# An encoder trunk on one core: widths of the FFNs' parts, pauses of the modulation sums, a second operand made from a copy, and row loads at another place

## The chip, the cores and the metric

The kernel runs on one core of a Trainium2 chip, in one launch. The metric is the time of an execution on the device in microseconds (us), as the median of several runs. The engines are named as in the profile: PE is TensorE (PEld its weight loads), DVE is VectorE, ACT is ScalarE, POOL is GpSimd, SP is SyncE, which here issues nearly all DMAs.

## The reference

A sequence of 256 positions of width 1024 passes two layers of three sub-layers each. Each sub-layer modulates its input with a scale and a shift that depend on a vector c, applies f, adds the result times a gate to the residual and normalises:

```
mod = silu(c) @ w_ada[l] + b_ada[l]              # nine vectors of 1024 per layer
h = x * (1.0 + scl) + shift
x = layer_norm(ALPHA * x + w * gate * f(h), ln_g, ln_b)
```

The six f are, in order: a SwiGLU FFN (0,0), a gMLP with a 128x128 position mixing, an FFN (0,1); then an FFN (1,0), an attention over chunks, an FFN (1,1). An FFN is `(silu(g) * u) @ w_down` with g, u the halves of `h @ w_gu`, 1024 to 2 x 2816 to 1024. Behind FFN (0,1) the residual stream is modulated a second time, with other vectors, into the operand from which attention's keys and values are made. Everything is float32.

## The kernel before, in words

**Split operands.** A float32 matmul is made from three fp32r matmuls: with x = xh + xl and w = wh + wl the kernel adds xh wh, xh wl and xl wh (`mm_unit`, L268). So every weight tile of 128 x 1024 (a unit) is loaded by a DMA (`load_raw`, L130; six buffers), cast by ACT (`hi`, L216) and subtracted by DVE (`lo`, L226). The 328 units stand in one list, `stream`, in the order of their use.

**Tiles and ticks.** The 256 rows are two row tiles t of 128. A pass (`gemm_pass`, L309) runs one row tile over 4, 6, 8 or 2 units; the same units then serve row tile 1. One unit for one row tile is six matmuls of 512 columns, and behind them comes a *tick* (L295). An FFN (`ffn`, L627) is cut into parts of columns of its inner width: for each part it makes the activations in chunks of 512 or 256 columns (`gu_part`, L483), then multiplies them by their rows of `w_down` (`down`, L611, in pieces of up to eight units) and adds the product to the residual X (`add_y`, L384, on DVE). An FFN has 132 ticks, 16 for a chunk of 512, 8 for one of 256, two for a unit of `w_down`; the gMLP has 96, attention 64; of the first FFN the first two chunks run in a form of their own, without ticks of this kind. The last piece of eight units runs with one half of the columns after the other (`half`), in 16 ticks called quiet.

**The planner.** All engines' orders are written out by hand while the ticks are counted. A tick runs what `after(n, fn)` has put off by n ticks, then makes as many lo (with their loads and casts) as the lead of six units (eight in the last piece) asks for (`prep`, L230), bounded by 11 unit buffers, then perhaps one *sum* (`run_sums`, L193). A sum is one eighth of a modulation vector: a 512 KB load on SP and a multiply with accumulation on DVE (`column`, L140, one instruction and a short read of the accumulator). There are 144, in the order of `SUMS`; when they run is set by the pairs (ticks, rate) given to `step` (L923): each tick adds its rate to a credit capped at 2; a tick that made a lo needs a credit of 2 for a sum, another one of 1; a quiet tick runs none. `need` (L198) runs missing sums at once, where a vector is wanted. A finished gate goes through DRAM and comes back as a row tile, loaded on SP.

**A seam** is where one sub-layer ends and the next begins. At the end of a row tile DVE adds, makes statistics, normalises (`end_sublayer`, L447); 4.5 or 5 ticks later PE transposes half of X (`make_h`, L363), ACT makes hf = A x + B from PSUM in four pieces and casts it to the operand's high part, DVE subtracts for the low part (hl, L333, `modulated`, L350); the other half follows two ticks later. Row tile 0 ends eight ticks ahead of the seam. The residual itself gets its LayerNorm rows g and b later, in two pieces of two DVE operations (`residual_affine`, L433), `LAG_R` ticks behind the second half. At the end of FFN (0,1) `make_h` has two sets to make, for hT and for hkT (attention's key and value operand), one right after the other. The rows g and b (two loads of 512 KB on SP, `load_lnrow`, L424) are loaded in `next_affine` (L914), in front of the last down piece.

**After a chunk** ACT applies Silu (sg, L475), one tick later DVE multiplies (a, L479), three ticks later PE transposes the product (tp, L344), ACT casts it and DVE subtracts (th, tl).

In the trace the sub-layers begin at about 0, 202, 351, 542, 738 and 862 us.

Of the kernel before, what the change touches and what calls it, by code (L numbers as in the profile page):

```python
# [8 lines left out]
F32 = mybir.dt.float32  # L9
# [5 lines left out]
P = 128  # L15
# [4 lines left out]
D_FF = 2816  # L20
# [12 lines left out]
ENDS = [HALVES, (0, 512, 768, 1024)]  # L33
# [8 lines left out]
LAG_A = 3  # L42
LAG_H = (4.5, 5)
LAG_H2 = 2
LAG_R = ((12, 16), (12, 16))
LAG_S = 1
LAG_HL = 2
LAG_T = 1.5
LAG_V = ((5, 8, 28, 32), (5, 9, 30, 36))

# [16 lines left out]
def encoder_kernel(ctx, tc, a, out):  # L67
    nc = tc.nc
# [8 lines left out]
    bigp = pool("bigp", N_BIG)  # L77
# [172 lines left out]
    def row_units(w, k0, nk, c0=0):  # L250
        return [lambda raw, k=k: [(raw, w[k * P:(k + 1) * P, c0:c0 + D])]
                for k in range(k0, k0 + nk)]

    def gu_units(w, c0, wd):
        wv = w.rearrange("k (s f) -> k s f", s=2)
        if wd == 512:
            return [lambda raw, k=k: [(raw.rearrange("p (s n) -> p s n", s=2),
                                       wv[k * P:(k + 1) * P, :, c0:c0 + 512])] for k in range(KD)]

        def two(raw, k):  # L260
            rv = raw.rearrange("p (q s n) -> p q s n", q=2, s=2)
            return [(rv[:, q], wv[(k + q) * P:(k + q + 1) * P, :, c0:c0 + 256]) for q in range(2)]
        return [lambda raw, k=k: two(raw, k) for k in range(0, KD, 2)]
# [24 lines left out]
    def after(n, fn, early=False):  # L288
        late.append([n, fn, early])
# [60 lines left out]
    def modulated(tp, A, B, js, p, tag, store, lag):  # L350

        w = len(js) * P
        hf = sgp.tile([P, 512], F32, tag="sg", name=nm("hf"))
        for i, j in enumerate(js):
            sl = slice(i * P, (i + 1) * P)
            nc.scalar.activation(hf[:, sl], tp[:, sl], AF.Identity,  # L356
                                 bias=B[:, j:j + 1], scale=A[:, j:j + 1])
        hi = p.tile([P, 512], F32R, tag=tag, name=nm("hh"))
        lo = p.tile([P, 512], F32R, tag=tag, name=nm("hl"))
        split4(hf[:, :w], (hi[:, :w], lo[:, :w]),  # L360
               lambda: store.extend(tiles4(hi, lo, len(js))), lag)

    def make_h(t, half, mods_):  # L363

        js = range(half * 4, half * 4 + 4)
        tp = pt.tile([P, 512], F32, tag="pt", name=nm("hp"))
        for i, j in enumerate(js):
            nc.tensor.transpose(tp[:, i * P:(i + 1) * P], X[t][:, j * P:(j + 1) * P], ident)  # L368
        for i, (A, B, p, tag, store) in enumerate(mods_):
            modulated(tp, A, B, js, p, tag, store[t], LAG_HL + 1.5 * i)  # L370

    def affine(scl, shift, ln):

# [26 lines left out]
    def pieces(x_, cuts):  # L400
        return [x_[:, c0:c1] for c0, c1 in zip(cuts, cuts[1:])]
# [20 lines left out]
    lnrow = {}  # L422

    def load_lnrow(ln):  # L424
        g = rowp.tile([P, D], F32, tag="lng", name=nm("lng"))
        b = rowp.tile([P, D], F32, tag="lnb", name=nm("lnb"))
        nc.sync.dma_start(out=g, in_=a["ln_g"][ln:ln + 1, :].partition_broadcast(P))
        nc.sync.dma_start(out=b, in_=a["ln_b"][ln:ln + 1, :].partition_broadcast(P))
        lnrow[ln] = (g, b)
# [1 line left out]
    waiting = [[], []]  # L431

    def residual_affine(t, ln):  # L433
        g, b = lnrow[ln]

        def part(sl):
            nc.vector.tensor_tensor(X[t][:, sl], X[t][:, sl], g[:, sl], op=ALU.mult)
            nc.vector.tensor_tensor(X[t][:, sl], X[t][:, sl], b[:, sl], op=ALU.add)
            waiting[t].remove(sl)
        waiting[t] = [slice(i * 512, (i + 1) * 512) for i in range(2)]  # L440
        for lag, sl in zip(LAG_R[t], waiting[t]):
            after(lag, lambda sl=sl: part(sl))
# [4 lines left out]
    def end_sublayer(t, stats, ln, nxt):  # L447

        mu, rs = stats.rstd()
        for x_ in pieces(X[t], HALVES):  # L450
            nc.vector.tensor_scalar(x_, x_, mu, rs, op0=ALU.subtract, op1=ALU.mult)
        hT[t] = []
        after(LAG_H[t], lambda: make_h(t, 0, nxt["mods"]))

        def second():
            make_h(t, 1, nxt["mods"])
            residual_affine(t, ln)
        after(LAG_H[t] + LAG_H2, second)

    def last_y(t, gate, first, done, cuts=HALVES):  # L460
# [166 lines left out]
    def ffn(l, i, gate, done, before_last, parts, start=None, cuts=(HALVES, HALVES)):  # L627
        for pi, part in enumerate(parts):
            aT = [[], []]
            if start and pi == 0:  # L630
                first_gu_part(a["ffn_gu"][l, i], part[:2], aT)
                start()
                gu_part(part[2:], aT)
            else:
                gu_part(part, aT)
            last = pi == len(parts) - 1
            down(sum(w for _, w in part) // P, aT, gate, pi == 0,
                 done if last else None, before_last if last else None,
                 cuts if last else (HALVES, HALVES))

    def ffn_stream(l, i, parts, skip=0):

        for pi, part in enumerate(parts):
            for c0, wd in part[skip if pi == 0 else 0:]:
                stream.extend(gu_units(a["ffn_gu"][l, i], c0, wd))
            stream.extend(row_units(a["ffn_down"][l, i], part[0][0] // P,
                                    sum(w for _, w in part) // P))

    PARTS1 = [[(c, 512) for c in (0, 512, 1024)], [(1536, 512), (2048, 512), (2560, 256)]]
    PART_A = [(0, 512), (512, 256)]  # L650
    PARTS2 = [PART_A, [(c, 512) for c in range(768, D_FF, 512)]]
# [103 lines left out]
    def transposed(accs, scale, name, store):  # L755
# [7 lines left out]
        for n in range(2):  # L763
            s_ = sgp.tile([P, 512], F32, tag="sg", name=nm(name))
            nc.scalar.mul(s_, accs[n], scale)
            after(LAG_T + n, lambda n=n, s_=s_: turn(n, s_))

# [4 lines left out]
    def attention(gate, done, before_last):  # L772
# [43 lines left out]
        def scores(t, hs):  # L816
# [22 lines left out]
            def second():  # L839
# [4 lines left out]
                st[(t, hs)] = pr  # L844
            after(LAG_T, second)

# [67 lines left out]
    def next_affine(ln, nxt, *keys):  # L914

        def f():
            need(*(k for ks in keys for k in ks))
            nxt["mods"] = [affine(mods[s_], mods[b_], ln) + dst
                           for (s_, b_), dst in zip(keys, ((htp, "h", hT), (bigp, "b", hkT)))]
            load_lnrow(ln)  # L920
        return f

    def step(ln, *rate):  # L923

        ada["rate"] = list(rate)
        nxt = {}
        return lambda t, stats: end_sublayer(t, stats, ln, nxt), nxt
# [10 lines left out]
    def start():  # L938
        for lag, fn in ((12, lambda: load_x(0)), (18, lambda: load_x(1)), (40, load_small)):
            after(lag, fn)  # L940

    ffn_stream(0, 0, PARTS1, 2)
    gmlp_stream()
    ffn_stream(0, 1, PARTS2)
    ffn_stream(1, 0, PARTS3)
    attention_stream()
    ffn_stream(1, 1, PARTS2)

    with tc.manual_schedule(engines={ET.SP, ET.PE, ET.DVE, ET.Activation, ET.Pool}):
        done, nxt = step(0, (6, 0), (16, 0.55), (0, 0.38))  # L950
        ffn(0, 0, (0, 2), done, next_affine(0, nxt, ((0, 4), (0, 3))), PARTS1, start=start)
        done, nxt = step(1, (4, 0), (16, 0.3), (24, 0), (0, 0.34))
        gmlp((0, 5), done, next_affine(1, nxt, ((0, 7), (0, 6))))
        done, nxt = step(2, (4, 0), (16, 0.5), (0, 0.34))
        ffn(0, 1, (0, 8), done, next_affine(2, nxt, ((1, 1), (1, 0)), (("kv", 1), ("kv", 0))), PARTS2)
        done, nxt = step(3, (4, 0), (16, 0.45), (0, 0.24))
        ffn(1, 0, (1, 2), done, next_affine(3, nxt, ((1, 4), (1, 3))), PARTS3)
        done, nxt = step(4, (4, 0), (0, 0.4))
        attention((1, 5), done, next_affine(4, nxt, ((1, 7), (1, 6))))
        step(5, (2, 0), (0, 0.8))  # L960
        ffn(1, 1, (1, 8), final, lambda: load_lnrow(5), PARTS2, cuts=ENDS)


# [38 lines left out]
```

## Time and profile before

| | |
|---|---|
| median of 3 runs | 1062.37 us (1062.26 to 1067.6) |
| the profiled execution | 1062.69 us |
| its span, first to last instruction | 1060.9 us |
| mean granted clock of TensorE | 0.996 |
| matmuls and weight loads | 4774 each |
| DMA | 285.74 MB, mean 269 GB/s |
| loads of units and sums | 160 of w_cols (sums), 160 and 32 of ffn_gu, 88 of ffn_down, 80 of the other weights |

The profile is of one execution. Busy time of an engine is the union of its instructions. Matmuls overlap each other and so do the instructions of DVE and ACT by some 0.1 us, so the cost of an instruction in a full queue is read from start to start. A wait is idle time of an engine, put down to the instruction whose semaphore came last.

### The profile page before, as it was taken

The page shows a single profiled execution, that of the slowest core. Times are in us where ns is not written, and L with a number is a line of the kernel's source. Part 1 is how long each engine was busy: PE and PEld are TensorE (multiplying, and loading weights), DVE is VectorE, ACT ScalarE, POOL GpSimd, SP SyncE. Part 2 cuts the span into 40 slices and gives each one's busy share as a digit, 9 for nine tenths or more (in the row PEclk, how much of TensorE's full clock was granted, in tenths as well). Part 3 has the DMA queues.
Part 4 walks back from the last instruction along what each step waited for, and adds up shares of the span by engine and source line. Part 5 has one row for each costly group of instructions (what it writes and reads, how often), then busy time and mean ns, then how long its engine had stood idle before and what let it go on. Part 6 is the DMA issues. An engine that isn't in the chain of part 4 may idle for free.

```text
span 1060.9 us, 13486 instructions
## 1 busy us (share of the span) xinstructions
PE 1030.3 (97%) x4774; PEld 839.6 (79%) x4774; DVE 856.8 (81%) x1224; ACT 506.1 (48%) x710; POOL 18.9 (2%) x41
## 2 busy tenths in 40 slices
PE   8999999999999999999988999999999999999996
PEld 6888887778887777888876788888887777888886
DVE  6898997799998899887778977877977778754555
ACT  4563344455433734444465444445656545444430
POOL 0000000001000000000000000000000000000000
PEclk9999999999999999999999999999999999999998
DMA  9999999688888589999937987885888638756541
GB/s 355 379 355 371 367 351 338 201 279 276 264 299 273 191 307 335 343 308 313 362 105 258 317 316 255 298 301 205 303 312 265 201 101 295 246 173 197 176 143 40
DMA packets 111347, 285.74 MB, mean 269 GB/s; under 512 B 9904, under 2 KB 22832, under 8 KB 111280
## 3 DMA queue, kind: packets, MB, share of 16 engines
q1 hardware_dynamic: 105648, 279.62, 75.8%
q10 hardware_dynamic: 5440, 5.24, 1.6%
q8 instruction: 37, 0.61, 0.2%
q14 instruction: 30, 0.25, 0.1%
q0 software_dynamic: 192, 0.02, 0.0%
HBM read 283.78 MB, written 1.07 MB: 268 GB/s over the span
## 4 chain that ended last, share of the span: by engine, by line
PE 68%; DVE 16%; DMA 6%; issue 5%; ACT 3%; SPq 0%; POOL 0%; POOLq 0%; DVEq 0%; ACTq 0%
PE acc L280 20%; PE acc L283 20%; PE acc L281 19%; DVE lo L226 6%; DVE raw L142 4%; DMA raw<-w_cols 3%; PE tp L344 2%; PE acc L530 1%; PE acc L532 1%; PE acc L534 1%; ACT hf L356 1%; PE sc L826 1%; ACT hi L216 1%; DMA raw<-ffn_down 1%; DMA raw<-ffn_gu 1%
## 5 line engine op out<-in xcount | busy, mean ns | idle before, releaser
L216 ACT CAST hi<-raw 128x1024 fp32r<-128x1024 f32 x328 | 337.6, 1051 | 211.6 <-DMA raw<-ffn_gu 70.3
L226 DVE TENSOR_TENSOR lo<-raw,hi 128x1024 fp32r<-128x1024 f32 x328 | 394.2, 1219 | 29.7 <-ACT hi L216 22.6
L280 PE MATMUL acc<-hi,hh 128*128 128x512 f32 x864 | 343.3, 397 | 0.0
L281 PE MATMUL acc<-lo,hh 128*128 128x512 f32 x864 | 337.6, 391 | 3.8 <-DVE lo L226 3.6
L283 PE MATMUL acc<-hi,hl 128*128 128x512 f32 x864 | 273.0, 391 | 4.1 <-DVE hl L333 3.9
L142 DVE CUSTOM_DVE_ANT_0 raw<-raw,c_row,bcol 128x1024 f32<-128x1024 f32 x160 | 203.9, 1278 | 10.3 <-DMA raw<-w_cols 8.0
L283 PEld LDWEIGHTS acc<-hi,hl 128*128 128x128 f32 x864 | 161.5, 188 | 42.0 <-DVE hl L333 7.9
L281 PEld LDWEIGHTS acc<-lo,hh 128*128 128x128 f32 x864 | 162.4, 188 | 38.2 <-DVE lo L226 6.6
L280 PEld LDWEIGHTS acc<-hi,hh 128*128 128x128 f32 x864 | 162.3, 188 | 33.7 <-issue 1.7
L280 PE MATMUL acc<-hi,th 128*128 128x512 f32 (+1 forms) x432 | 167.4, 388 | 0.4 <-ACT hi L216 0.4
L281 PE MATMUL acc<-lo,th 128*128 128x512 f32 (+1 forms) x432 | 164.4, 382 | 1.5 <-DVE lo L226 1.5
L283 PE MATMUL acc<-hi,tl 128*128 128x512 f32 (+1 forms) x432 | 142.9, 382 | 0.0
L281 PEld LDWEIGHTS acc<-lo,th 128*128 128x128 f32 x432 | 81.3, 188 | 17.0 <-DVE lo L226 2.1
L330 ACT CAST th<-tp 128x512 fp32r<-128x512 f32 (+1 forms) x56 | 31.1, 556 | 131.7 <-PE tp L344 131.6
L280 PEld LDWEIGHTS acc<-hi,th 128*128 128x128 f32 x432 | 81.2, 188 | 16.0 <-ACT hi L216 1.2
L283 PEld LDWEIGHTS acc<-hi,tl 128*128 128x128 f32 x432 | 80.6, 188 | 16.0
L333 DVE TENSOR_TENSOR tl<-tp,th 128x512 fp32r<-128x512 f32 (+1 forms) x56 | 36.1, 648 | 52.5 <-ACT th L330 52.5
L356 ACT ACTIVATE hf<-hp,B,A 128x128 f32<-128x128 f32 x96 | 36.0, 454 | 62.8 <-PE hp L368 52.0
L479 DVE TENSOR_TENSOR a<-acc,sg 128x512 f32<-128x512 f32 (+1 forms) x48 | 30.7, 643 | 40.9 <-ACT sg L475 40.8
L393 DVE TENSOR_TENSOR gy<-acc,gate 128x512 f32<-128x512 f32 (+1 forms) x49 | 33.1, 675 | 25.6 <-PE acc L283 25.6
L475 ACT ACTIVATE sg<-acc 128x512 f32<-128x512 f32 (+1 forms) x48 | 26.6, 559 | 39.9 <-PE acc L283 39.8
L344 PE MATMUL tp<-ident,a 128*128 128x128 f32 x176 | 27.2, 274 | 8.8 <-DVE a L479 8.8
(101 smaller groups left out, 618.5 us busy)
## 6 DMA issues: line engine op xcount, KB each, us to landing
raw<-w_cols SPq DMA_DIRECT2D x160, 512.0 KB, 5.2
raw<-ffn_gu SPq DMA_DIRECT2D x160, 512.0 KB, 5.5
raw<-ffn_down SPq DMA_DIRECT2D x88, 512.0 KB, 4.8
raw<-w_in SPq DMA_DIRECT2D x32, 512.0 KB, 6.6
raw<-ffn_gu SPq DMA_DIRECT2D x32, 256.0 KB, 4.3
raw<-w_out SPq DMA_DIRECT2D x16, 512.0 KB, 4.7
raw<-w_kv SPq DMA_DIRECT2D x16, 512.0 KB, 6.3
raw<-w_q SPq DMA_DIRECT2D x8, 512.0 KB, 4.9
```

The costliest lines, as they stand in the source:

```text
L142: nc.vector.tensor_tensor_reduce(out=raw, in0=raw, in1=c_row, scale=1.0, scalar=bcol[:, ci, j:j + 1], op0=ALU.mult, op1=ALU.add, accum_out ...
L216: nc.scalar.copy(hi, raw)
L226: nc.vector.tensor_tensor(lo, raw, hi.bitcast(F32), op=ALU.subtract)
L280: nc.tensor.matmul(acc, lhsT=xh, rhs=wh[:, sl], start=k == 0, stop=False)
L281: nc.tensor.matmul(acc, lhsT=xh, rhs=wl[:, sl], start=False, stop=False)
L283: nc.tensor.matmul(acc, lhsT=xl, rhs=wh[:, sl], start=False, stop=k == nk - 1)
L330: nc.scalar.copy(hi, src)
L333: nc.vector.tensor_tensor(lo, src, hi.bitcast(F32), op=ALU.subtract)
L344: nc.tensor.transpose(tp[:, q * P:(q + 1) * P], src[:, q * P:(q + 1) * P], ident)
L356: nc.scalar.activation(hf[:, sl], tp[:, sl], AF.Identity, bias=B[:, j:j + 1], scale=A[:, j:j + 1])
L393: nc.vector.tensor_tensor(tmp, acc[:, :w], mods[gate][:, sl], op=ALU.mult)
L479: nc.vector.tensor_tensor(av[:, :wd], u, sg[:, :wd], op=ALU.mult)
```

## The change

It sets the FFNs (0,1) and (1,1) to the parts that (0,0) has (1536 and 1280 columns in place of 768 and 2048), and (1,0) to 1024, 768 and 1024 in place of 768, 1024 and 1024. It sets other rates and longer first pauses for the sums. The two pieces of the residual's affine run 18 and 22 ticks behind the second `make_h` in place of 12 and 16. The rows g and b are loaded 8 ticks behind the second `make_h` of row tile 0 in place of in front of the last down piece (the last sub-layer keeps its place). In `make_h` the second set, where there is one, is made 8 ticks later, from a copy of the transposed tile that ACT writes to SBUF (pool "b", 18 buffers), and its split waits one tick.

```diff
-LAG_R = ((12, 16), (12, 16))
+LAG_R = ((18, 22), (18, 22))
+LAG_K = 8
+LAG_W = 8
...
-        for i, (A, B, p, tag, store) in enumerate(mods_):
-            modulated(tp, A, B, js, p, tag, store[t], LAG_HL + 1.5 * i)
+        (A, B, p, tag, store), *others = mods_
+        modulated(tp, A, B, js, p, tag, store[t], LAG_HL)
+        if others:
+            xs = bigp.tile([P, 512], F32, tag="b", name=nm("xs"))
+            nc.scalar.copy(xs, tp)
+        for A, B, p, tag, store in others:
+            after(LAG_K, lambda A=A, B=B, p=p, tag=tag, store=store:
+                  modulated(xs, A, B, js, p, tag, store[t], LAG_S))
...
     def residual_affine(t, ln):
-        g, b = lnrow[ln]
-
         def part(sl):
+            g, b = lnrow[ln]
...
             residual_affine(t, ln)
+            if t == 0:
+                after(LAG_W, lambda: load_lnrow(ln))
...
-    PART_A = [(0, 512), (512, 256)]
-    PARTS2 = [PART_A, [(c, 512) for c in range(768, D_FF, 512)]]
-    PARTS3 = [PART_A, PARTS2[1][:2], PARTS2[1][2:]]
+    PARTS2 = [[(0, 512), (512, 512)], [(1024, 512), (1536, 256)], [(1792, 512), (2304, 512)]]
...
-            load_lnrow(ln)
...
-        done, nxt = step(0, (6, 0), (16, 0.55), (0, 0.38))
+        done, nxt = step(0, (6, 0), (16, 0.55), (0, 0.55))
-        done, nxt = step(1, (4, 0), (16, 0.3), (24, 0), (0, 0.34))
+        done, nxt = step(1, (24, 0), (8, 0.3), (20, 0), (0, 0.25))
-        done, nxt = step(2, (4, 0), (16, 0.5), (0, 0.34))
-        ffn(0, 1, (0, 8), done, next_affine(2, nxt, ((1, 1), (1, 0)), (("kv", 1), ("kv", 0))), PARTS2)
-        done, nxt = step(3, (4, 0), (16, 0.45), (0, 0.24))
-        ffn(1, 0, (1, 2), done, next_affine(3, nxt, ((1, 4), (1, 3))), PARTS3)
-        done, nxt = step(4, (4, 0), (0, 0.4))
+        done, nxt = step(2, (18, 0), (0, 0.42))
+        ffn(0, 1, (0, 8), done, next_affine(2, nxt, ((1, 1), (1, 0)), (("kv", 1), ("kv", 0))), PARTS1)
+        done, nxt = step(3, (22, 0), (0, 0.33))
+        ffn(1, 0, (1, 2), done, next_affine(3, nxt, ((1, 4), (1, 3))), PARTS2)
+        done, nxt = step(4, (12, 0), (0, 0.47))
...
-        step(5, (2, 0), (0, 0.8))
-        ffn(1, 1, (1, 8), final, lambda: load_lnrow(5), PARTS2, cuts=ENDS)
+        step(5, (18, 0), (0, 0.3))
+        ffn(1, 1, (1, 8), final, lambda: load_lnrow(5), PARTS1, cuts=ENDS)
```

## Rows read from the trace of the kernel before

**Rows 1.** The page: busy time by engine, and one group of weight loads

```profile
PE 1030.3 (97%) x4774; PEld 839.6 (79%) x4774; DVE 856.8 (81%) x1224; ACT 506.1 (48%) x710; POOL 18.9 (2%) x41
...
L281 PEld LDWEIGHTS acc<-lo,hh 128*128 128x128 f32 x864 | 162.4, 188 | 38.2 <-DVE lo L226 6.6
```

**Rows 2.** Windows: busy us and (instructions) of each engine, PEclk, DMA share, GB/s

```profile
440.00:460.00 20.00, 20.00 (x93) 16.55 (x92) 16.11 (x20) 9.45 (x12) 0.00 (x0) 1.00 0.93 323
535.00:600.00 65.00, 57.31 (x262) 45.96 (x261) 55.17 (x78) 40.80 (x69) 1.13 (x2) 1.00 0.67 225
740.00:760.00 20.00, 20.00 (x98) 16.56 (x97) 19.10 (x27) 13.93 (x24) 1.16 (x3) 1.00 0.84 288
```

**Rows 3.** Waits of PEld, 60:180 and 176:190: us, times, longest

```profile
PEld acc L281 <- DVE lo L226: 0.8, 1, 0.8
...
PEld acc L281 <- DVE lo L226: 1.1, 1, 1.1
PEld acc L280 <- ACT hi L216: 0.8, 1, 0.8
```

**Rows 4.** Waits of PEld, 225 to 240 and 300 to 345

```profile
PEld acc L281 <- DVE lo L226: 3.2, 2, 2.4
...
PEld acc L281 <- DVE lo L226: 1.7, 2, 1.1
```

**Rows 5.** Waits of PEld, 345 to 420

```profile
PEld acc L281 <- DVE lo L226: 1.6, 2, 1.1
PEld tp L344 <- issue: 1.5, 1, 1.5
PEld tp L344 <- DVE a L479: 1.3, 1, 1.3
PEld acc L283 <- DVE hl L333: 1.1, 2, 0.6
```

**Rows 6.** Waits of PEld, 535 to 600

```profile
PEld tp L344 <- DVE a L479: 4.6, 2, 2.7
PEld acc L283 <- DVE hl L333: 3.7, 2, 2.5
```

**Rows 7.** Waits of PEld, 860 to 900

```profile
PEld tp L344 <- DVE a L479: 2.9, 2, 1.8
PEld acc L283 <- DVE hl L333: 2.0, 3, 1.0
```

**Rows 8.** Timeline of DVE, 370 to 374: start, us, instruction

```profile
370.13 0.68 DVE L437 TENSOR_TENSOR X<-X,lng 128x512 f32<-128x512 f32 x1
...
371.45 1.28 DVE L142 CUSTOM_DVE_ANT_0 raw<-raw,c_row,bcol 128x1024 f32<-128x1024 f32 x1
...
372.66 1.22 DVE L226 TENSOR_TENSOR lo<-raw,hi 128x1024 fp32r<-128x1024 f32 x1
373.80 0.68 DVE L333 TENSOR_TENSOR tl<-tp,th 128x512 fp32r<-128x512 f32 x1
```

**Rows 9.** Windows of line L142 alone (the sums): DVE busy us and (instructions)

```profile
357.00:390.00 33.00, 11.56 (x18) 1.00 0.80 273
...
57.00:202.00 145.00, 41.19 (x64) 1.00 0.92 336
```

**Rows 10.** Timeline of ACT, 557 to 561

```profile
557.97 1.50 ACT L356 ACTIVATE hf<-hp,B,A 128x128 f32<-128x128 f32 x4
...
560.03 1.50 ACT L356 ACTIVATE hf<-hp,B,A 128x128 f32<-128x128 f32 x4
```

**Rows 11.** The chain that ended last, 170 to 190: start us, us, what

```profile
172.00 9.31 DMA raw<-ffn_down
```

**Rows 12.** Windows in the first FFN

```profile
88.00:178.00 90.00, 89.59 (x405) 73.76 (x404) 80.74 (x106) 39.26 (x45) 1.73 (x3) 1.00 0.97 348
84.00:89.00 5.00, 5.00 (x25) 4.15 (x24) 3.75 (x6) 2.33 (x3) 0.00 (x0) 1.00 1.02 408
```

More of the change, by code (lines that the diff above doesn't have):

```diff
@@ L943, in encoder_kernel @@
     gmlp_stream()
-    ffn_stream(0, 1, PARTS2)
-    ffn_stream(1, 0, PARTS3)
+    ffn_stream(0, 1, PARTS1)
+    ffn_stream(1, 0, PARTS2)
     attention_stream()
-    ffn_stream(1, 1, PARTS2)
+    ffn_stream(1, 1, PARTS1)
     with tc.manual_schedule(engines={ET.SP, ET.PE, ET.DVE, ET.Activation, ET.Pool}):
-        done, nxt = step(0, (6, 0), (16, 0.55), (0, 0.38))
+        done, nxt = step(0, (6, 0), (16, 0.55), (0, 0.55))
         ffn(0, 0, (0, 2), done, next_affine(0, nxt, ((0, 4), (0, 3))), PARTS1, start=start)
-        done, nxt = step(1, (4, 0), (16, 0.3), (24, 0), (0, 0.34))
+        done, nxt = step(1, (24, 0), (8, 0.3), (20, 0), (0, 0.25))
         gmlp((0, 5), done, next_affine(1, nxt, ((0, 7), (0, 6))))
-        done, nxt = step(2, (4, 0), (16, 0.5), (0, 0.34))
-        ffn(0, 1, (0, 8), done, next_affine(2, nxt, ((1, 1), (1, 0)), (("kv", 1), ("kv", 0))), PARTS2)
-        done, nxt = step(3, (4, 0), (16, 0.45), (0, 0.24))
-        ffn(1, 0, (1, 2), done, next_affine(3, nxt, ((1, 4), (1, 3))), PARTS3)
-        done, nxt = step(4, (4, 0), (0, 0.4))
+        done, nxt = step(2, (18, 0), (0, 0.42))
[3 more added lines that the diff above has]
+        done, nxt = step(4, (12, 0), (0, 0.47))
         attention((1, 5), done, next_affine(4, nxt, ((1, 7), (1, 6))))
-        step(5, (2, 0), (0, 0.8))
-        ffn(1, 1, (1, 8), final, lambda: load_lnrow(5), PARTS2, cuts=ENDS)
+        step(5, (18, 0), (0, 0.3))
+        ffn(1, 1, (1, 8), final, lambda: load_lnrow(5), PARTS1, cuts=ENDS)
 def kernel(x, c, w_ada, b_ada, ln_g, ln_b, ffn_gu, ffn_down, gmlp_w_in, gmlp_b_in, gmlp_ln_g,
```

## The prediction

> **What bounds the kernel now.** I read the page's engine line first [rows 1]: TensorE (PE) counts as busy for 97% of the span, VectorE (DVE) for 81%, ScalarE (ACT) for 48%. Since matmuls overlap, I use the weight loads (PEld) as the meter. One takes 188 ns [rows 1], and in an undisturbed stretch they fill 16.55 of 20 us [rows 2]; so one 512-column matmul starts every 188 x 20 / 16.55 = 227 ns, and a tick (six of them) lasts 1.36 us. A stretch with less PEld than 82.75% has lost time: 535 to 600 should hold 53.8 us, holds 45.96, and so lost 7.8 / 0.8275 = 9.5 us. 740 to 760, also behind a seam, lost nothing [rows 2]. Granted clock is 1.00 in all of them, so the clock is no part of this.
>
> The list of waits says what these losses are. They sit in four of the five seams and at two last down pieces: in the first FFN 0.8 and 1.9 us [rows 3]; in the gMLP 3.2, then 1.7 [rows 4]; behind the next seam 5.5 [rows 5]; behind the one where attention's key/value operand is made 9.8 (8.3 [rows 6], and the line of 1.5 on issue, word for word as in [rows 5]); behind attention 4.9 [rows 7]. That is 28 us. The releaser is nearly always DVE (lo, a, hl): it comes late, because its own queue is full.
>
> **The change, part by part.** Durations are starts to starts on a DVE that never idles [rows 8]: the two operations of a residual piece 371.45 - 370.13 = 1.32 us, a sum 372.66 - 371.45 = 1.21, a lo 373.80 - 372.66 = 1.14.
>
> *Pauses, seam by seam.* From 357 to 390 DVE ran 18 instructions of sums, two per sum: nine sums, 10.9 us of a 33 us stretch [rows 9]. With (18,0) instead of (4,0) the six or seven before tick 18 go: about 8 us. The waits there are 1.3 and 1.5 (transposes of a) and, once the first add_y lies on top, 1.6 (lo) [rows 5]: 4.4 us in all, less than the 8 us freed. The wider first part also moves that add_y from tick 36 to 64 and 72. Gain 4.4. In the gMLP five sums (6.0 us) leave ticks 4 to 20, and the pieces of row tile 1 move from ticks 19 and 23 to 25 and 29; the waits of 3.2 us lie at 225 to 240 (ticks 17 to 28), just behind them. Gain 3.2. Later in the gMLP the rate is 0.25 from tick 52 instead of 0.34 from tick 44, some five sums (6 us) fewer before tick 72: the 1.7 goes. Behind attention (18,0) replaces (2,0) at 0.8: the 2.9 on a goes; of 2.0 on hl the 1.1 stays that the seam at 345 shows without any sum [rows 5, 7]: 3.8.
>
> *Second operand.* Today ACT makes hkT right behind hT: four hf and one cast, 560.03 - 557.97 = 2.06 us each [rows 10], four times, in front of the casts that PE waits for. Afterwards a copy (about 0.5 us, by the cast of the same size: 2.06 less the 1.50 of the four hf) stands there, and the 2.06 us come 8 ticks later. Hl falls from 3.7 to the 1.1 of the other seam, 2.6; the waits on a and the one booked as issue (4.6 + 1.5) go with the sums except about 1.0, since two of the late sets come at ticks 5 and 7, ahead of the first Silu at tick 8: 5.1. Together 7.7. The bounds: 0 if ACT's order merely shifts the wait, 8.7 if hl alone stays.
>
> *Row loads.* Two loads of 512 KB now stand in front of the last down pieces of weights. One weight took 9.31 us to land there [rows 11] and cost 1.9 us [rows 3]. Moved to 6.5 ticks behind a seam they are issued by SP ahead of raws that are needed ten ticks later, on a queue that no sum uses then, and are read 10 ticks (13.6 us) after: cost nothing. If that cover is gone, 2 x 1.29 = 2.6 us per seam.
>
> *Where the sums go.* Counting credits tick by tick (a tick that makes a lo needs 2, others 1, cap 2) gives 32, 17, 41, 30, 17 and 7 sums per sub-layer before; the trace has 64 instructions, so 32, in the first [rows 9]. Afterwards 39, 10, 41, 31, 17 and 6. So the first FFN takes seven more. Its queue moved 348 GB/s at share 0.97 and DVE was busy 80.74 of 90 us [rows 12]. Seven sums are 8.5 us of DVE against 9.3 us idle, and 7 x 524,288 B at the 408 GB/s reached at 84 to 89 [rows 12], 1.29 us each, 9.0 us of queue. Lower end: the idle time takes it all and the waits of rows 3 vanish, -2.7. Upper end: all of the queue's time is felt, +9.0. I take +4.4, above the middle, because a lead that already ran out twice [rows 3] leaves little to absorb it.
>
> By the Trainium skill (DMA: Bandwidth & Descriptors, section Where 436 GB/s comes from) transfers between HBM and SBUF are bound near 358 GB/s, by which each of the seven costs 1.46 us, 10.2 in all; the 408 GB/s of rows 12 speaks against it.
>
> *Widths.* Matmuls, transposes (22 per row tile), loads and add_y keep their numbers; two FFNs keep two parts, the third three. The last part has 10 instead of 16 rows of units, so fewer matmuls are split in halves; the columns are the same: 0, within 0.5 either way.
>
> **Sum.** -3.2 - 1.7 - 4.4 - 7.7 - 3.8 + 4.4 = -16.4 us. The profiled execution took 1062.69 us (span 1060.9), 0.3 above the median of 1062.37; so 1046.3 for it and **1046** for the median.
>
> **Rivals.** *The first FFN's queue is full.* If 348 GB/s is the ceiling there, seven loads cost 7 x 1.51 = 10.5 us, and in the second FFN (0.92 loads per tick, 1.39 us against 1.36) another 1: 1062.4 - 20.8 + 11.5 = 1053. For it: share 0.97; against it: 408 GB/s for 5 us at a share only a little higher. By the page's 358 GB/s it would be near the same. 0.13.
>
> *The seams are made by the burst itself*: eight units in the first eight ticks, where DVE needs eight lo and the chain of the other row tile. Then only rows and copy gain (1.9 + 2.6) and the first FFN pays: about 1060 to 1062. Against it: 740 to 760, the same burst with nothing lost [rows 2]. With this goes the case that the change does nothing of what it says, because a late operand makes the flush run everything at once: the last half of row tile 1 is stored at tick 9 and used at 12, so it should not. Together 0.10, no difference.
>
> *Slower: the sums are only moved.* Between ticks 16 and 36 DVE now meets 20 x 0.57 of lo, 18 x 0.42 x 1.21 of sums, four pieces of 1.32 and three pairs of a and tl at 1.2: 11.4 + 9.1 + 5.3 + 3.6 = 29.4 us in 27.2. If the 2.2 us too much are not covered by a lead built before tick 18 (10 ticks x (1.36 - 0.57 - 0.15) = 6 us on paper), each seam loses the same as now, only 15 ticks later, and the first FFN's 9.0 come on top, less the 1.9 of the rows: 1069.5. It decides when the lead at tick 16 is under 2 us. 0.07.
>
> **Numbers.** Forecast 0.70, own range 1040 to 1055. A measurement of this kernel can tell about 0.5%, 5.3 us: faster (below 1057) is the forecast and the full queue, 0.83; same 0.10; slower 0.07. The range 1040 to 1057: its low end is the sum with the first FFN at its lower end (1038.9) held back by 1.1 for seams that go only in part; its high end takes in the full queue and a loss of 9.0 with two thirds of the seams' gain.
>
> **What would show it.** PEld near 82.75% at 345 to 420 and behind attention; waits on a gone, those on hl at 1.1 per seam; no weight with 9 us to landing before the last pieces; DVE above 85 of 90 us in the first FFN with more waits on lo there, that FFN longer by 2 to 9 us. I am wrong if waits on lo or a reappear 25 to 40 ticks behind the seams, or if the first FFN grows by over 12 us.

## The result and the profile after

The changed kernel takes 1051.48 us in the median of four runs (1051.25 to 1051.9). The kernel before, run beside it, took 1063.59 us (four runs, 1062.26 to 1067.6). The ratio is 0.988, with a 95% interval of 0.9851 to 0.9909. So it is faster by some 12 us (10 to 16 by the interval), where 16.4 were forecast. The profiled executions differ by a little less: the span went from 1060.9 to 1050.0 us, 10.9 us. All that follows is reckoned from spans, since only they can be split into stages. Medians are of the fast executions; one execution each of u_rates, u_rows and f_32 took 1666 to 2094 us and is left out.

The page of the changed kernel: its first line, busy times, and the group of weight loads that answers to [rows 1].

```profile
span 1050.0 us, 13437 instructions
...
PE 1030.0 (98%) x4756; PEld 840.0 (80%) x4756; DVE 856.1 (82%) x1224; ACT 506.0 (48%) x714; POOL 18.7 (2%) x41
...
L283 PEld LDWEIGHTS acc<-lo,hh 128*128 128x128 f32 x864 | 162.4, 188 | 37.8 <-DVE lo L228 6.2
```

Every engine is busy for as long as before (DVE 856.1 against 856.8 us); only the span shrank. The change took nothing off an engine: it filled gaps. And the costliest group of idle time, weight loads that wait for a lo, stayed as large (6.2 against 6.6 us), though the gaps behind the seams went. Those 6.2 us are new ones, at other places.

Windows of the changed kernel (the columns of [rows 2]):

```profile
440.00:460.00 20.00, 20.00 (x90) 16.57 (x89) 19.47 (x27) 7.39 (x8) 0.00 (x0) 1.00 0.93 340
535.00:600.00 65.00, 63.64 (x293) 51.66 (x291) 52.38 (x67) 44.11 (x71) 1.13 (x2) 1.00 0.67 219
...
88.00:178.00 90.00, 87.12 (x391) 70.95 (x390) 82.48 (x110) 36.02 (x40) 1.84 (x3) 1.00 0.98 366
```

An undisturbed stretch is the same (16.57 us of weight loads in 20). From 535 to 600 the weight loads rose from 45.96 to 51.66 us, so by the prediction's own meter the loss fell from 9.5 to (53.8 - 51.66) / 0.8275 = 2.6 us. In the first FFN it went the other way: 73.76 became 70.95 [rows 12], (73.76 - 70.95) / 0.8275 = 3.4 us more lost in those 90.

The waits of the weight loads in the changed kernel (us, times, longest), window by window: 60 to 205, the first FFN; 205 to 300, the gMLP (none from 300 to 345); 345 to 420; 535 to 600; 600 to 640; 725 to 852, attention; 850 to 900.

```profile
PEld acc L283 <- DVE lo L228: 6.4, 5, 2.4
...
PEld acc L285 <- DVE hl L335: 1.1, 2, 0.6
PEld acc L283 <- DVE lo L228: 0.6, 1, 0.6
...
PEld acc L285 <- DVE hl L335: 1.1, 2, 0.6
...
PEld acc L285 <- DVE hl L335: 1.6, 2, 1.0
PEld tp L346 <- DVE a L489: 1.3, 2, 1.0
...
PEld acc L283 <- DVE lo L228: 1.1, 1, 1.1
...
PEld pT L862 <- ACT pTs L864: 1.6, 1, 1.6
PEld acc L283 <- DVE lo L228: 1.5, 2, 0.8
...
PEld acc L285 <- DVE hl L335: 1.0, 2, 0.6
```

Against [rows 3 to 7]: behind the seams an hl of about 1.0 is what stays, as forecast, and behind the one with two operands 1.6 and 1.3 on a. The waits on lo have gone to three places where there were none or few: the first FFN (6.4 us), the middle of FFN (1,0) (1.1) and attention (1.5, with 1.6 on pTs).

The lengths of the stages say the same in one number each. A stage begins at the start of the first matmul on its first unit in the timeline; a sub-layer's last piece is counted with it. Lengths in us, of the kernel before, the one after, and those experiments that are told below:

| | first FFN | gMLP | FFN (0,1) | FFN (1,0) | attention | FFN (1,1) to its last piece | span |
|---|---|---|---|---|---|---|---|
| before | 144.7 | 149.0 | 191.3 | 195.7 | 123.9 | 168.8 | 1060.9 |
| after | 148.9 | 144.5 | 187.6 | 190.0 | 127.1 | 164.8 | 1050.0 |
| difference | +4.2 | -4.5 | -3.7 | -5.7 | +3.2 | -4.0 | -10.9 |
| u_rates | 143.3 | 147.6 | 188.7 | 191.5 | 123.9 | 169.6 | 1051.9 |
| u_rates_aff | 143.7 | 147.4 | 190.2 | 193.6 | 123.9 | 170.2 | 1056.7 |
| w_alone | 145.4 | 148.5 | 191.6 | 196.1 | 123.9 | 167.1 | 1061.3 |
| u_parts | 151.5 | 144.4 | 197.9 | 197.6 | 127.2 | 165.1 | 1071.4 |
| u_copy | 150.5 | 144.5 | 187.6 | 193.7 | 127.1 | 164.8 | 1055.9 |
| u_rows | 154.2 | 144.5 | 188.4 | 189.9 | 126.0 | 164.8 | 1054.8 |
| u_affine | 149.8 | 144.0 | 187.7 | 189.6 | 127.2 | 164.8 | 1050.2 |
| f_32 | 143.4 | 150.9 | 187.6 | 191.2 | 125.7 | 164.9 | 1052.8 |
| u_att | 149.3 | 144.5 | 187.6 | 189.9 | 125.0 | 164.8 | 1049.1 |
| best1 | 143.2 | 150.9 | 187.6 | 192.0 | 123.9 | 164.8 | 1049.3 |
| best2 | 143.3 | 149.6 | 196.6 | 189.0 | 123.9 | 164.8 | 1054.4 |
| best3 | 143.2 | 150.1 | 189.5 | 190.2 | 124.6 | 164.8 | 1051.9 |

What is left out (the start, and the end behind the last FFN's 168.8 or 164.8) changes by up to about 2 us between kernels. The first FFN with the new rate comes out between 148.9 and 151.5 us in kernels that have the very same program up to there, so in that column a difference of 2 us from after means nothing. Each row is one profile, and in some of them TensorE's granted clock fell behind a wait: in FFN (1,0) of w_alone, u_parts, u_copy and u_rates_aff, in FFN (1,1) of u_rates_aff, in FFN (0,1) of u_parts and best2, in the gMLP of best2 and best3, in the first FFN of u_copy and u_rows. Where the rows are shown below, such a fall adds 1.7 to 3.0 us that are not a wait. In the stages of before, after, u_rates, u_affine, f_32, u_att and best1 the clock was 1.00 throughout.

### The profile page after: what moved, and what is told of

The parts are those of the page before. It is cut to its first block, busy times and chain, and to the rows that moved or that the text cites. A ratio compares the mean times of both kernels' runs of the same rounds, so it can differ in the third digit from the quotient of the medians.

```text
span 1050.0 us, 13437 instructions
## 1 busy us (share of the span) xinstructions
PE 1030.0 (98%) x4756; PEld 840.0 (80%) x4756; DVE 856.1 (82%) x1224; ACT 506.0 (48%) x714; POOL 18.7 (2%) x41
## 4 chain that ended last, share of the span: by engine, by line
PE 64%; DVE 15%; DMA 11%; issue 5%; ACT 4%; SPq 1%; POOL 0%; POOLq 0%; DVEq 0%; ACTq 0%
PE acc L285 20%; PE acc L283 20%; PE acc L282 20%; DVE lo L228 5%; DMA raw<-w_cols 4%; DMA raw<-ffn_gu 4%; DVE raw L144 4%; PE tp L346 2%; DMA bias<-rel 1%; ACT hi L218 1%; ACT hf L358 1%; DVE st L420 1%; PE sp L731 1%; PE hp L371 1%; DVE gy L402 1%
## 5 line engine op out<-in xcount | busy, mean ns | idle before, releaser
L144 DVE CUSTOM_DVE_ANT_0 raw<-raw,c_row,bcol 128x1024 f32<-128x1024 f32 x160 | 204.1, 1280 | 13.2 <-DMA raw<-w_cols 11.5
L358 ACT ACTIVATE hf<-hp,B,A 128x128 f32<-128x128 f32 x80 | 30.1, 456 | 63.7 <-PE hp L371 52.9
```

What stands on the lines that cost most here:

```text
L144: nc.vector.tensor_tensor_reduce(out=raw, in0=raw, in1=c_row, scale=1.0, scalar=bcol[:, ci, j:j + 1], op0=ALU.mult, op1=ALU.add, accum_out ...
L358: nc.scalar.activation(hf[:, sl], tp[:, sl], AF.Identity, bias=B[:, j:j + 1], scale=A[:, j:j + 1])
```

## The experiments

Each of the kernels is the changed one with one part undone, unless it is said otherwise. The ratios are to the kernel before.

**The pauses and rates alone (u_rates).** The six lists go back to those of before; widths, copy, affine and rows stay as changed.

```diff
-step(0, (6, 0), (16, 0.55), (0, 0.55))
+step(0, (6, 0), (16, 0.55), (0, 0.38))
-step(1, (24, 0), (8, 0.3), (20, 0), (0, 0.25))
+step(1, (4, 0), (16, 0.3), (24, 0), (0, 0.34))
-step(2, (18, 0), (0, 0.42))
+step(2, (4, 0), (16, 0.5), (0, 0.34))
-step(3, (22, 0), (0, 0.33))
+step(3, (4, 0), (16, 0.45), (0, 0.24))
-step(4, (12, 0), (0, 0.47))
+step(4, (4, 0), (0, 0.4))
-step(5, (18, 0), (0, 0.3))
+step(5, (2, 0), (0, 0.8))
```

> The changed kernel with the six old rate lists of step (pauses of 2 to 4 ticks, first FFN at 0.38 again); everything else as changed. Theory (the pauses carry the seams' gain): waits on lo and a come back behind the seams, 3.2 us in the gMLP at about tick 25, 4.4 behind the next seam, about 5 behind the one with two operands, 2.9 behind attention, some 1 late in the gMLP; the first FFN gives back its 4.2 and the two waits on its last piece: about +10 on 1051.5, so 1060 to 1064. Rival (affine, row loads, copy and widths carry it): at most 1053, or below 1051 because the first FFN is relieved.

Measured: 1054.96 us, ratio 0.9914 (0.9886 to 0.9942). That is below all that the theory of the sums as the seams' cause allowed, and above what the rival allowed (1053): some three quarters of the gain stay without any new pause. The sums behind the seams, windows of their line: u_rates first, then after, at 350 to 388, 538 to 580, 850 to 880.

```profile
350.00:388.00 38.00, 11.56 (x18) 1.00 0.89 312
538.00:580.00 42.00, 10.29 (x16) 1.00 0.83 289
850.00:880.00 30.00, 8.15 (x13) 1.00 0.75 256
```

```profile
57.00:206.00 149.00, 50.26 (x78) 1.00 0.92 343
350.00:388.00 38.00, 3.86 (x6) 1.00 0.74 240
538.00:580.00 42.00, 2.57 (x4) 1.00 0.72 232
850.00:880.00 30.00, 1.29 (x2) 1.00 0.70 233
```

The pauses do what they say: nine, eight and six sums behind the seams become three, two and one, and the first FFN holds 78 instructions, 39 sums, as counted from the credits. But u_rates, with nine sums in front of PE at 351, waits there for little (waits of the weight loads, 345 to 420, 530 to 600 and 850 to 900):

```profile
PEld tp L346 <- DVE a L489: 1.3, 2, 0.8
PEld acc L285 <- DVE hl L335: 1.1, 2, 0.6
PEld acc L283 <- DVE lo L228: 0.3, 1, 0.3
...
PEld tp L346 <- DVE a L489: 3.9, 3, 2.0
...
PEld tp L346 <- DVE a L489: 3.7, 1, 3.7
```

Of the 5.5 us of [rows 5] 2.7 are left, though the sums are all there. By the table the pauses and rates give -3.1 us in the gMLP, -1.1 in FFN (0,1), -1.5 in FFN (1,0) and -4.8 in FFN (1,1), 10.5 together; they cost +5.6 in the first FFN and +3.2 in attention. Net 1.7 by the stages, 1.9 by the spans; by the ratios, which do not rest on the profiled execution alone, 3.6 (0.988 against 0.9914). That the sums are the seams' only cause falls with this: at 351 and 542 something else of the change had already made the room.

**The widths, alone and taken back (w_alone, u_parts).** w_alone is the kernel before with the new widths and nothing else; u_parts is the changed kernel with the old widths.

```diff
-PART_A = [(0, 512), (512, 256)]
-PARTS2 = [PART_A, [(c, 512) for c in range(768, D_FF, 512)]]
-PARTS3 = [PART_A, PARTS2[1][:2], PARTS2[1][2:]]
+PARTS2 = [[(0, 512), (512, 512)], [(1024, 512), (1536, 256)], [(1792, 512), (2304, 512)]]
```

(so in w_alone, with FFNs (0,1) and (1,1) on PARTS1 and (1,0) on PARTS2; in u_parts the other way round)

> The kernel before with the FFNs in the new parts, nothing else. Theory (widths pay by where the first add_y lies, with the pauses and also a little without): the second FFN without its last piece falls from 168.6 to about 166 us, the third by 0 to 1 from 172.5, the last by 0 to 1 from 168.8, the rest as before: 1058 to 1061 in all. Rival (widths are worth nothing without the pauses, as predicted): within 1.5 of 1062.4.

> The changed kernel with the FFNs in their old parts (first part 768 columns in the second, third and last FFN); rates, pauses, copy, rows and affine as changed. Theory (wider first parts carry the rest of the gain behind the seam at 351 us, where pauses gave only 1.0 of 3.7): the second FFN without its last piece goes from 164.9 back to 166 to 168, with waits on a of the 256-column chunk and on lo behind the early add_y; in the third FFN one sum of the gate is forced at tick 36 and its gate comes late, 1 to 3 us; last FFN +0 to 1: 1054 to 1058. Rival (widths do nothing, the affine does): within 1 of 1051.5.

Measured: w_alone 1063.17 us, ratio 0.9988 (0.9969 to 1.0007), no difference, as its rival had it (the 1.7 us that it gains in FFN (1,1) are matched by a longer start and first FFN and by a fallen clock in FFN (1,0)). u_parts 1069.34 us, ratio 1.0065 (1.0041 to 1.0089), beyond both expectations: all the rest of the change with the old widths is slower than the kernel before. FFN (0,1) is 10.3 us longer than after, FFN (1,0) 7.6. DVE's timeline of u_parts around 402 shows why (in brackets the idle time before, and its releaser):

```profile
402.68 0.17 DVE L167 TENSOR_SCALAR mod<-mod 128x8 f32<-128x8 f32 x1
409.16 0.69 DVE L402 TENSOR_TENSOR gy<-acc,gate 128x512 f32<-128x512 f32 x1 [6.31 <-DMA gate<-grow]
```

The first add_y multiplies by the sub-layer's gate (0,8). Its sums are the next in the list, and a pause of 18 ticks makes them end later; at 402.68 the finished vector is made up (L167), then goes through DRAM, and with a first part of 768 columns add_y is due before the gate is back (for row tile 0 at tick 30: 24 ticks of chunks and six units; the 36 of the prediction is row tile 1's). DVE runs in order and stands for 6.3 us with every lo behind it. PE's waits there, 395 to 425:

```profile
PEld acc L283 <- DVE lo L228: 7.5, 2, 5.0
```

The wait of 5.0 us also cost TensorE's clock (windows of u_parts; the third column from the right is the granted clock):

```profile
404.00:409.00 5.00, 5.00 (x24) 4.14 (x23) 0.00 (x0) 0.00 (x0) 0.00 (x0) 1.00 0.54 181
409.00:414.00 5.00, 0.75 (x4) 0.28 (x2) 4.77 (x7) 1.04 (x1) 0.00 (x0) 0.78 1.02 395
414.00:419.00 5.00, 4.70 (x12) 3.65 (x13) 5.00 (x8) 2.10 (x2) 0.00 (x0) 0.54 0.98 320
```

At 0.54, almost at its lower level of 1.2 GHz, PE began 12 matmuls in 4.70 us where 24 went in 5.00 before: 0.46 x 5 = 2.3 us more. With the 7.5 that is 9.8 of the 10.3. So the wider first part is worth nothing by itself and yet it carries the pauses: it puts the first add_y behind the gate. It does so with little to spare. In the changed kernel itself, FFN (1,0), with a first part of 1024 and a pause of 22, has the same wait of DVE (600 to 625):

```profile
DVE gy L402 <- DMA gate<-grow: 4.5, 1, 4.5
```

Here the lead covers most of it; PE's 1.1 us at 600 to 640, shown above, is what gets through. In best2, where the rate in this FFN is higher and DVE has no wait on the gate, PE's wait on lo is 0.2 and the FFN takes 189.0 instead of 190.0.

**The second operand (u_copy).** Both sets are made at once again, from PSUM.

```diff
-        (A, B, p, tag, store), *others = mods_
-        modulated(tp, A, B, js, p, tag, store[t], LAG_HL)
...
-            nc.scalar.copy(xs, tp)
...
+        for i, (A, B, p, tag, store) in enumerate(mods_):
+            modulated(tp, A, B, js, p, tag, store[t], LAG_HL + 1.5 * i)
```

> The changed kernel with both operand sets made at once again, from PSUM, with the old split lags. Theory: only the seam at 538 us changes; the wait on hl there goes from 1.6 to about 3.7 us and the first wait on a (0.96) to 2 or 3, the later ones stay small because no sum runs: 1053.5 to 1056. Rival (the copy only shifts ACT's work): 1051 to 1052.

Measured: 1056.34 us, ratio 0.9929 (0.9906 to 0.9951). FFN (1,0) grew by 3.7 us, as much as was expected of that stage, but only half of it by waits; of the span's other 2.2 us 1.6 are the first FFN's scatter. The waits of its weight loads, 530 to 600:

```profile
PEld acc L285 <- DVE hl L335: 2.6, 1, 2.6
PEld tp L346 <- DVE a L483: 1.9, 1, 1.9
```

The wait on hl of [rows 6] comes back in part, 2.6 where after has 1.6; that on a (L483 in this kernel) is 1.9 where after has 1.3. With lo (1.3 against 1.1) the waits of this FFN are 1.8 us longer. Behind the wait on hl the clock fell as well, which it did not in the kernel before behind one as long (windows of u_copy):

```profile
543.00:546.00 3.00, 3.00 (x9) 2.38 (x10) 2.93 (x5) 2.94 (x8) 0.00 (x0) 0.65 0.86 306
546.00:549.00 3.00, 3.00 (x11) 2.37 (x11) 2.20 (x6) 2.73 (x3) 0.55 (x1) 0.78 0.82 284
```

0.35 x 3 + 0.22 x 3 = 1.7 us. On ACT in the changed kernel the copy stands where the second set stood (timeline of after):

```profile
548.43 0.58 ACT L376 COPY xs<-hp 128x512 f32<-128x512 f32 x1
548.90 1.05 ACT L218 CAST hi<-raw 128x1024 fp32r<-128x1024 f32 x1
549.85 1.65 ACT L358 ACTIVATE hf<-xs,B,A 128x128 f32<-128x128 f32 x4
```

0.47 us from start to start, as estimated (0.5); the four hf from SBUF take 1.65 instead of 1.50. The copy, with the later second set that it allows, is thus worth about 2 us of waits, and 3.7 us only in a profile in which the clock falls behind them.

**The rows' loads (u_rows).** They go back in front of the last down piece.

```diff
-            if t == 0:
-                after(LAG_W, lambda: load_lnrow(ln))
...
+            load_lnrow(ln)
```

> The changed kernel with the row loads in front of the last down piece again. Theory: the first FFN's last piece, which now waits 2.7 us, waits about 2.6 more, the other last pieces 0 to 0.5: 1053 to 1055. If the loads at their new place cost something in the attention stage (3.2 us longer than before), that stage gets 1 to 3 us shorter, and the total is 1051 to 1053.

Measured: 1059.13 us, ratio 0.9956 (0.9942 to 0.9971), the dearest part after the widths and above both expectations. The first FFN is 5.3 us longer, 4.4 of them in its last piece; the other FFNs at most 0.8, and attention is 1.1 shorter, its wait on pTs 0.8 instead of 1.6: so the loads cost a little at their new place. Waits of the weight loads, 176 to 206, of u_rows and then of after:

```profile
PEld acc L283 <- DVE lo L228: 3.0, 3, 1.1
PEld acc L282 <- ACT hi L218: 2.8, 1, 2.8
```

```profile
PEld acc L283 <- DVE lo L228: 2.8, 3, 1.0
```

The waits differ by 2.8 us only, a weight that comes late behind the rows. The rest is the clock (windows of u_rows):

```profile
186.00:190.00 4.00, 1.13 (x4) 0.30 (x2) 1.21 (x2) 1.04 (x1) 0.00 (x0) 1.00 1.01 391
190.00:194.00 4.00, 3.21 (x7) 2.33 (x8) 3.95 (x4) 3.14 (x3) 0.00 (x0) 0.64 1.02 413
194.00:198.00 4.00, 4.00 (x18) 3.27 (x17) 2.84 (x4) 0.00 (x0) 0.00 (x0) 0.93 0.92 348
```

0.36 x 4 + 0.07 x 4 = 1.7 us. So the loads, worth 1.9 by [rows 3] and 1.4 in u_rates (143.3 against 144.7, which also has them moved), cost about 4.5 in front of a first FFN that runs at the new rate, 1.7 of it by the clock. That the lead is used up when they come fits this and was not tested.

**The affine, with the pauses and without (u_affine, u_rates_aff).** Both set the two pieces back to 12 and 16 ticks; u_rates_aff has the old pauses as well, as u_rates.

```diff
-LAG_R = ((18, 22), (18, 22))
+LAG_R = ((12, 16), (12, 16))
```

> The changed kernel with the residual's pieces 12 and 16 ticks behind the second half again. Theory: without sums DVE has room at ticks 10 to 23, so within 0.7 of 1051.5, and the waits at ticks 25 to 45 (0.55 in the gMLP, 1.1 in the fourth sub-layer) go, not more. Rival (the later affine carries part of the seams' gain): waits on a come back at ticks 12 to 24 of three seams, 1054 to 1058.

> u_rates with the residual's pieces at 12 and 16 again. If the later affine carries what neither the pauses (1.0) nor the widths alone (1.1) gave behind the seam at 351 us: second FFN without its last piece 165.9 to about 167.5, and 0.5 to 1.5 more in the third and last FFN, 1055 to 1059. If not: the stages as in u_rates within 0.5.

Measured: u_affine 1052.15 us, ratio 0.9889 (0.9866 to 0.9912), span 1050.2 against 1050.0: nothing. u_rates_aff 1058.5 us, ratio 0.9945 (0.9925 to 0.9964), span 4.8 us above u_rates: 1.5 in FFN (0,1), 2.1 in FFN (1,0), 0.6 in FFN (1,1), in sum what its first expectation had; but only the 1.5 are waits. By the ratios it is 3.3, and their intervals overlap. In FFN (1,0) the waits are the same in both, 5.8 us in all, and in FFN (1,1) u_rates_aff waits less (5.3 against 6.1); what it has more there is the clock, which fell in it (to 0.65 at 575, to 0.58 at 877) and not in u_rates. The waits of u_rates_aff at 345 to 420 are longer:

```profile
PEld acc L283 <- DVE lo L228: 1.6, 1, 1.6
PEld tp L346 <- DVE a L489: 1.3, 1, 1.3
PEld acc L285 <- DVE hl L335: 1.1, 2, 0.6
```

They are those of [rows 5] again but for the one on issue. Without the pauses the later affine takes away the wait on lo (0.3 in u_rates) and leaves that on a (1.3). With the pauses both are gone at either place of the affine. So behind this seam the later affine and the pauses are two ways to clear the same DVE stretch: the pauses give 2.5 us with the affine at its old place (u_rates_aff against u_affine) and 1.1 with it later (u_rates against after).

**Where the first FFN's seven sums go (f_32).** The old rate in the first FFN, and a higher one at the end of the gMLP, so that about seven sums move there.

```diff
-step(0, (6, 0), (16, 0.55), (0, 0.55))
+step(0, (6, 0), (16, 0.55), (0, 0.38))
-step(1, (24, 0), (8, 0.3), (20, 0), (0, 0.25))
+step(1, (24, 0), (8, 0.3), (20, 0), (0, 0.52))
```

> The changed kernel with the first FFN at rate 0.38 again (32 sums instead of 39) and the gMLP's last rate 0.52 instead of 0.25 (16 sums instead of 10). Theory (seven sums too many cost the first FFN 4 to 6 us): the first FFN falls from 148.9 to about 143.3 us; the gMLP, 144.5, grows by 0 to 4 as its late ticks take six sums more: 1046 to 1050. Rival (the first FFN is longer for another reason): it stays over 147.

Measured: 1053.6 us, ratio 0.9908 (0.9886 to 0.993). The first FFN gives back 5.5 us as its theory said, but the gMLP takes 6.4 where 0 to 4 were expected. Waits of the weight loads of f_32, 205 to 350:

```profile
PEld acc L283 <- DVE lo L228: 6.4, 5, 2.1
```

The same total on lo as the changed kernel has in the first FFN, at another place. Seven sums cost 0.8 us of PE's time each in the first FFN (5.5 / 7; 1.2 by the longest first FFN at the new rate, 151.5). Six of them went to the gMLP and cost 1.1 each there (6.4 / 6).

**Attention's rate (u_att), and combinations (best1, best2, best3).** u_att sets attention's list back; best1 is u_att with f_32's two edits. best2 and best3 look for a cheaper split: they have u_rates' lists in the first FFN and the gMLP, and for the rest best2 has the lists of the second fence, best3 those of the third.

```diff
-step(4, (12, 0), (0, 0.47))
+step(4, (4, 0), (0, 0.4))
```

```diff
-step(2, (18, 0), (0, 0.42))
+step(2, (18, 0), (0, 0.5))
-step(3, (22, 0), (0, 0.33))
+step(3, (24, 0), (0, 0.4))
-step(4, (12, 0), (0, 0.47))
+step(4, (12, 0), (0, 0.12))
```

```diff
-step(2, (18, 0), (0, 0.42))
+step(2, (18, 0), (0, 0.45))
-step(3, (22, 0), (0, 0.33))
+step(3, (18, 0), (0, 0.4))
-step(4, (12, 0), (0, 0.47))
+step(4, (12, 0), (0, 0.2))
```

> The changed kernel with the attention's old rates (4,0), (0,0.4). Theory (a higher rate in fewer ticks puts sums between the scores' operations): the attention falls from 127.1 to about 124 us, 1047.5 to 1049 in all. Rival (the later row loads or affine lengthen it): it stays at 127.

> f_32 and u_att together. If the two costs are independent: first FFN about 143.3, attention about 124, gMLP 144.5 to 148.5, the rest as changed: 1042 to 1047. If a stage only hands its sums' cost to the next, 1048 to 1052.

> The changed kernel with the old rates in the first FFN and the gMLP, (18,0), (0,0.5) in the second FFN, (24,0), (0,0.4) in the third, (12,0), (0,0.12) in the attention: sums 32, 17, 49, 37, 4, 5. Theory (sums cost nothing only in the second and third FFN behind their pause): first FFN 143.3, gMLP 147.6, second FFN 187.6 to 189, third 188.5 to 191 with its gate in time (no wait of DVE on the gate, 1.1 us of lo less), attention 122 to 124, last FFN 186.5: 1043 to 1047. Rival (the sums' cost follows them into the second and third FFN): 1048 to 1053.

> The changed kernel with the old rates in the first FFN and the gMLP, (18,0), (0,0.45) in the second FFN, (18,0), (0,0.4) in the third (its gate is summed at tick 23 instead of 37), (12,0), (0,0.2) in the attention; sums 32, 17, 44, 39, 8, 4. If 0.42 to 0.45 is still free in the second FFN and 0.4 in the third: first FFN 143.3, gMLP 147.6 to 150, second FFN 187.6 to 189.5, third 189 without a wait of DVE on the gate, attention 123.9, last 186.5: 1045 to 1049 in all. If 0.45 is already too much: second FFN 191 or more, with a wait over 3 us on lo and half the granted clock behind it, 1050 to 1056.

Measured: u_att 1051.14 us, 0.9886 (0.9869 to 0.9903); best1 1051.61 us, 0.9895 (0.9874 to 0.9915); best2 1056.16 us, 0.9919 (0.9892 to 0.9947); best3 1052.69 us, 0.9878 (0.9857 to 0.99). None is better than the changed kernel by more than its interval. u_att shortens attention by 2.1 us, to 125.0, between its theory's 124 and its rival's 127: the wait on pTs, 1.6 above, is gone, and 1.1 on lo stays. best1 has attention at 123.9, as before (u_att runs 18 sums in attention, best1 17; whether that is why u_att keeps its 1.1 was not settled), but pays 6.4 in the gMLP and 2.0 in FFN (1,0); its rival, that a stage only hands the cost of its sums on (1048 to 1052), is what came. best2 lies above both of its expectations, best3 between 1050 and 1056, where its second one put it, without that one's long wait in FFN (0,1). best2 shows the limit of FFN (0,1): at a rate of 0.5 it takes 8.3 us longer than at 0.42, up to its last piece. That is one wait of 3.3 us on lo at 463, and behind it the clock at 0.50 (windows of best2):

```profile
462.00:466.00 4.00, 1.13 (x6) 0.63 (x5) 3.96 (x7) 1.86 (x2) 0.00 (x0) 0.89 0.83 322
466.00:472.00 6.00, 6.00 (x15) 4.61 (x16) 6.00 (x9) 1.28 (x2) 0.00 (x0) 0.50 0.97 336
```

Further waits of 2.3 us on a and 1.1 on lo lie in the same FFN.

## Why the prediction was right, and where it was too high

The sign and the range held (1051.5 in 1040 to 1057). The gain was put 5.5 us too high against the spans: 16.4 where 10.9 came. Term by term, by the stages:

- **Seam and end of the gMLP: -4.9 forecast, -4.5 measured.** Right. The waits of [rows 4] went, but for 0.6 us on lo and the 1.1 on hl at the seam. With the old pauses 3.1 of it is lost again, so here the pauses are the main cause.
- **Seam at 351: -4.4 forecast, -3.7 measured.** The waits on lo and a went as forecast; the cause was put too simply. With the rest of the change in place the pauses are worth 1.1. The later affine gives 1.5 without them and 0 with them, and the other 1.1 (191.3 to u_rates_aff's 190.2) lies with the widths, the rows and the copy; taken back one by one, the rows give 0.8 here and the copy 0. The prediction counted the affine's later place as a gain in the gMLP only, and gave it no term at this seam.
- **Seam at 542: -7.7 forecast, -5.7 measured.** hl came to 1.6 instead of 1.1, a to 1.3 instead of 1.0, and the wait for the gate, 1.1 us of PE's time, was not foreseen: 0.5 + 0.3 + 1.1 = 1.9 of the 2.0 missing. The shares differ too: the prediction gave 5.1 of its 7.7 to the waits on a and on issue, which were to go with the sums, but without the pauses only 1.5 is lost again. The copy's 2.6 was near: the waits are 1.8 longer without it.
- **Behind attention: -3.8 forecast, -4.0 measured.** Right, and with the old pause all of it is lost (4.8 against u_rates). The widths alone give 1.7 here (w_alone), which does not add to it.
- **First FFN: +4.4 forecast, +4.2 measured.** Right in the middle, as the balance of seven sums at 5.6 and the rows at 1.4; that it came within 0.2 is luck, since the same program took 148.9 to 151.5 us. DVE's busy time rose only to 82.48 us in the window where over 85 was forecast, while the DMA share stood at 0.98 and 366 GB/s. By the Trainium skill (DMA: Bandwidth & Descriptors, section Where 436 GB/s comes from) transfers between HBM and SBUF are bound near 358 GB/s; the 366 GB/s over these 90 us do not agree. Waits on lo were the sign, as said. A sum cost 0.8 us of PE's time (up to 1.2), less than the 1.29 us of queue or 1.21 of DVE that it takes, so part of it went into idle time. Which of the two it was, the prediction left open. The chain that ended last points to the queue: from 88 to 178 loads of sums and weights make 47.9% of it in after (29.4 + 12.2 + 6.3), where in u_rates, with 32 sums, those listed make 8.3%, and ACT's casts, which come before the lo, wait for weights (after, 88 to 178):

```profile
ACT hi L218 <- DMA raw<-ffn_gu: 26.9, 14, 4.4
ACT hi L218 <- DMA raw<-ffn_down: 15.2, 10, 3.1
```

In the kernel before these are 19.3 and 7.4 us.
- **Attention: 0 forecast, +3.2 measured.** This is the step that failed most. The prediction counted attention's 17 sums before and after and costed their move at nothing, since the number is equal. But they now run at 0.47 from tick 12 on instead of 0.4 from tick 4; the waits shown above, 1.6 on pTs and 1.5 on lo, make 3.1 of the 3.2. The old list takes back 2.1 (u_att). The rest is open: with the new list and 17 sums f_32 takes 125.7, 1.4 less than after, and without the rows' loads there u_rows takes 126.0. An equal number at a higher rate is not a cost of zero.
- **Widths: 0 forecast, 0 measured alone**, and about 18 us by the stages (10.3 + 7.6 + 0.3) when taken from under the pauses. The prediction named the tick of the first add_y (36 to 64; in truth 30 and 36 to 64 and 72 for the two row tiles) as a gain for the lo behind it, and did not ask when the gate that add_y reads is ready. The late gate is the wait that the pause adds, and the wider first part is what keeps PE from paying for it.
- **Row loads: nothing at their new place**, right behind the seams, which have no wait of their own with them; attention may pay up to 1.1 (u_rows). Their value at the old place depends on the first FFN's rate (1.4 to 5.3).

Of the rivals, the full queue's time (1053) is nearest to the result, and by half of its own way: the chain of the first FFN does point to the queue, but seven sums cost 5.6 us and not 10.5, and the second FFN, where it asked for 1 us more, became shorter. The slower rival, sums that are only moved, holds for the pauses' balance: what they gain behind the seams, 10.5 us, comes back as 8.8 in the first FFN and attention. Its mechanism (the seam's loss 15 ticks later) did not show: behind the seam at 351 the weight loads of the changed kernel have only the hl shown above up to 420, and from 420 to 538 no wait is listed. The case that the burst itself makes the seams' loss falls too: after the change the burst is the same, and behind three of the four seams only hl's 1.0 stays. So most of the net gain (by the ratios 9.1 of 12.8 us, by the spans 9.0 of 10.9) came with the copy, the rows' loads, the affine and the widths together, and the new pauses add 2 to 4 us on top; the intervals of after and u_rates overlap.

## What to carry to other kernels

When two edits clear the same stretch of an engine, price each with the other in place, not each against the kernel before. When work is held back, follow each value that it produces to its first reader and compare ticks, since a part that is worth nothing alone may be what keeps that reader from standing still. And work that a seam is freed of must be paid where it lands: look at rate and lead there, not at how often it runs.

## What the runs showed of the hardware

A long wait of TensorE can cost more than its length here. Behind PE's waits of 5.0 us (u_parts, 409), 3.3 us (best2, 463) and 4.0 us (best3, 256), and behind a run of 1.0, 1.0, 2.8 and 1.1 us within eight (u_rows, 184 to 191), the granted clock fell to 0.50 to 0.72 in the windows that followed, with 1.7 to 3.0 us more lost each time. The rows of best3:

```profile
256.00:260.00 4.00, 0.41 (x2) 0.28 (x2) 3.90 (x8) 3.69 (x5) 1.39 (x1) 1.00 0.82 255
260.00:266.00 6.00, 6.00 (x21) 4.79 (x21) 5.90 (x8) 1.05 (x3) 0.07 (x1) 0.72 0.74 227
```

The length of the wait does not decide it. In the kernel before, a wait of 2.7 us at 577 left the clock at 1.00; the same wait in w_alone took it to 0.63; one of 3.7 us in u_rates left it at 1.00 (windows of w_alone, then of u_rates):

```profile
580.00:583.00 3.00, 3.00 (x11) 2.48 (x12) 2.96 (x5) 1.66 (x3) 0.58 (x1) 0.63 0.90 300
...
874.00:877.00 3.00, 2.56 (x13) 2.19 (x14) 3.00 (x5) 1.47 (x3) 0.00 (x0) 1.00 0.73 270
```

u_rates, best2 and best3 have the same program up to the end of the gMLP, and PE waits 3.2, 3.6 and 4.0 us in them at the same place of it. The clock stayed at 1.00 in the first and fell in the other two, and the gMLP took 147.6, 149.6 and 150.1 us. So before a difference of two or three us between two profiles is put down to an edit, the clock behind each long wait has to be compared. What decides whether it falls was not looked for.
